# Two-layer diffusion backbone: the residual's latent rows are kept in DRAM during attention, the first output-weight unit is split early into their place, and GpSimd's subtracts leave the attention

## The chip, the cores and the metric

The kernel runs on one core of one Trainium2 chip. The metric is the device time of one execution in microseconds (us). The kernel before took 1191.76 us, the median of three runs (1187.81, 1191.76 and 1194.09). The core has five engines, each with a queue of its own that it serves in order: TensorE (PE in the profile, its weight loads PEld), VectorE (DVE), ScalarE (ACT), GpSimd (POOL) and SyncE (SP, which here issues the DMAs).

## The reference, cut to what matters

512 latent tokens and 256 context tokens of width 1024 go through two layers. Layer 0 mixes by pooling, layer 1 by attention with 8 query heads and 2 key/value heads of 128; each layer ends with a squared-ReLU MLP of width 4096. Only the latent stream leaves layer 1. The part around the change:

```python
# end of layer 0, both streams
x = x + gt2 * rms_norm(m_lat, g_mlp_post)
# layer 1
h_lat = modulate(rms_norm(x, g_mix_pre), sh1, sc1)
q_l, k_l, v_l = qkv_project(h_lat, w_qkv, g_q, g_k)      # and for the context
q_l, k_l = apply_axial_rope(q_l), apply_axial_rope(k_l)
s = einsum('bqhgd,bkhd->bhgqk', q, k) * HEAD_DIM ** -0.5  # 768 keys
p = softmax(s)
o = einsum('bhgqk,bkhd->bqhgd', p, v)
y_lat = o.reshape(B, L, D) @ w_o
x = x + gt1 * rms_norm(y_lat, g_mix_post)                 # residual: needs x again
m_lat = square(relu(modulate(rms_norm(x), sh2, sc2) @ w_mlp_in)) @ w_mlp_out
x = x + gt2 * rms_norm(m_lat, g_mlp_post)
```

The residual stream x is not needed between the normalisation that opens layer 1 and the addition behind the output projection.

## The kernel before, in words

Every fp32 operand of a large product is kept as two fp32r parts: hi is a rounded copy, lo is the operand minus hi. A product is then three matmuls (hi by hi, hi by lo, lo by hi). To make such a pair is called a split: one copy (ACT, or GpSimd) and one subtract (DVE, or GpSimd); `split`, lines 126 to 135, does it for a weight unit of 2048 columns, or for a quarter of one (512 columns) when `q` is given. With `pin` the two instructions keep the place that they have in the program.

The residual rows lie in one tile, `xr`, of six row blocks of 128 tokens: four latent (t = 0 to 3) and two context (4 and 5). It belongs to a pool, `residents`, on the right side of the on-chip memory together with `gate` and `junk`, which is closed while other tiles need the room (`held`), the rows going to the DRAM tile `spill` and back.

The order of the work is written by hand: `Steps` collects functions with planned times in us, sorts them by time and runs them, which emits the instructions. The framework then places the instructions that are not pinned by a simulated timeline (`TC_OPTS`, line 38), so what is ready earlier on an engine or on SP's queue may come ahead of what is written earlier. `last0` (line 1118) plans the end of layer 0 for the row blocks in the order 4, 5, 0, 1, 2, 3: residual add (`norm_r`), mean square (`norm_s`), scaled copy (`norm_c`), transposes with modulation (`norm_pair`), key/value projection (`kv_a` to `kv_c`), query projection (`q_a` at 67.851 to 104.478, `q_e`, `q_b` with the rotary products at line 1053). The attention's base is planned at 102.5, the output projection at 102.5 + 2.7 x 43.691.

`attention` has 32 steps of 2.7 planned us, head by head, four row blocks each. Step i computes scores (line 1204) into a two-bank PSUM tile (two of them), their negated maximum (DVE, line 1208), the exponential (ACT, line 1209) into one of four probability buffers `pbuf`, which are the first 768 columns of the two context row blocks of `xr`, of `gate` and of `acc`; the normalisation (line 1217 or 1219); six transposes (line 1229) whose results are split from PSUM (ACT line 1231, DVE line 1232); and, every second step, 18 matmuls of values by probabilities (line 1243), split again (lines 1245 and 1246). Transposes, query heads, values and projections share four PSUM banks.

The output weights w_o come in four units of 1 MB, (column half, row half), each loaded into one of three raw buffers and then split into a slot of the ring `aring` (line 1179): half of `hL` in `ra` (free once the query projections are done), `unit[0]`, `unit[1]`, `unit[2]`. The first two units are split in the attention, at steps 7 and 11.386, copy and subtract both on GpSimd and pinned:

```python
at(7, lambda: wo[0].append(wo_unit(0, 0, raws)))
at(7.01, lambda: split(*raws[0], True, True, True))
at(11.386, lambda: wo[0].append(wo_unit(0, 1, raws)))
at(11.396, lambda: split(*raws[1], True, True, True))
```

The other two go to slots that the attention itself uses and are split after it. `output` (line 1311) multiplies, evicts (`attn_ev`), adds the residual (`norm_r`, line 324), normalises, and starts the MLP; `mlp1` stores the four latent row blocks to `spill` (line 838), closes the residents, and gets the rows back before its end.

Of the kernel before, what the change touches and what calls it, by code (L numbers as in the profile page):

```python
# [9 lines left out]
F32 = mybir.dt.float32  # L10
F32R = mybir.dt.float32r
BF16 = mybir.dt.bfloat16
# [5 lines left out]
P = 128  # L18
D = 1024
# [21 lines left out]
class Steps:  # L41
# [3 lines left out]
    def at(self, t, fn, *args):  # L45
        self.items.append((t, len(self.items), fn, args))
# [7 lines left out]
def backbone(ctx: ExitStack, tc, x, c, ctx_in, c_ctx, w_ada, b_ada, g_mix_pre, g_mix_post,  # L54
# [10 lines left out]

    held = [ExitStack(), ExitStack()]

    def residents(stack):
        pool = stack.enter_context(tc.tile_pool(name="residents", bufs=1, side="right"))
        return (pool.tile([P, NT, D], F32, name="xr"), pool.tile([P, 2, D], F32, name="gate"),  # L70
                pool.tile([P, D], BF16, name="junk"))

    xr, gate, junk = residents(held[0])
    psA = ctx.enter_context(tc.tile_pool(name="psA", bufs=2, space=PSUM))
# [90 lines left out]
    def row_rstd(src):  # L165
        ss = sm_tile("ss")
        mean_square(src, ss, 0)
        return rstd(ss, 1)
# [151 lines left out]
    def gated(t, dst, src, n0, n1, pool=False):  # L320
        return (gp if pool else ve).tensor_tensor(out=dst[:, n0:n1], in0=src, in1=gate[:, slot[t], n0:n1], op=ALU.mult)  # L321

    def residual(t, y, n0=0, n1=D):
        ve.scalar_tensor_tensor(out=xr[:, t, n0:n1], in0=y[:, n0:n1], scalar=rs[t][:, 0:1],
                                in1=xr[:, t, n0:n1], op0=ALU.mult, op1=ALU.add)
# [157 lines left out]

    def norm_s(t, half=False):
        if not half:
            rs[t] = row_rstd(xr[:, t, :])
            return
        ss = sm_tile("ss")
        for h in range(2):
            mean_square(xr[:, t, 512 * h:512 * h + 512], ss, h)  # L490
        rs[t] = rstd(ss, 2)

    def norm_c(t, act, pool):
        r = rs[t][:, 0:1]
        if act:
            sc.activation(accv[:, t, :], xr[:, t, :], AF.Copy, scale=r)
        else:
            (gp if pool else ve).tensor_scalar(out=accv[:, t, :], in0=xr[:, t, :], scalar1=r, scalar2=None,
                                               op0=ALU.mult)

    turned = {}
# [333 lines left out]
    def mlp1(inner, last):  # L835
        nonlocal xr, gate, junk
        for t in range(NL):
            sy.dma_start(spill[:, t], xr[:, t])
        held[1].close()
        closing = ExitStack()  # L840
        pool = closing.enter_context(tc.tile_pool(name="pairs", bufs=1, side="right"))
# [276 lines left out]
    def last0(st, n, t):  # L1118
# [2 lines left out]
        st.at([8.8, 14, 19.2, 24.4, 29.6, 34.8][n], norm_r, t, (False, True, False, False, False, False)[n])  # L1121
        st.at([10, 16.738, 20.4, 25.6, 30.8, 36][n], norm_s, t, (False, False, False, False, True, False)[n])
        st.at([12, 17.906, 22.4, 27.6, 32.8, 36.716][n], norm_c, t, (True, True, True, True, True, True)[n], (False, False, False, False, False, False)[n])
        if n % 2:
            st.at([18.2, 28.6, 39][n // 2], norm_pair, t - 1, 1, 0, hH, hL, True, (True, True, False)[n // 2],
                  ((True, False, False, False, False, False, False, True), (True, True, True, False, False, False, True, True), (True, False, True, False, True, False, True, False))[n // 2])
# [49 lines left out]
    pTH = unit[2][:, 0:NT * LAT].rearrange("p (s n) -> p s n", n=LAT)  # L1176
    pTL = unit[1][:, 0:NT * LAT].rearrange("p (s n) -> p s n", n=LAT)
    pbuf = lambda i: (xr[:, 4, 0:TOK], xr[:, 5, 0:TOK], gate[:, 1, 0:TOK], acc[:, 4 * D:4 * D + TOK])[i]
    aring = Ring([ra[:, 8192:12288], unit[0], unit[1], unit[2]])

    def wo_unit(ch, kk, wait=None):
        return aring.load(w_o[0, 512 * kk:512 * kk + 512, 512 * ch:512 * ch + 512]
                          .rearrange("(k p) n -> p k n", p=P), 512, True, wait)

    steps = [(h, t) for h in range(NQ) for t in range(NL)]
# [95 lines left out]

    first1 = []

    def attention(st, base, unit_t):
        at = lambda i, fn, *args: st.at(base + unit_t * i, fn, *args)
        for i, (h, t) in enumerate(steps):
            if t == 0:
                at([-2, 3, 4.542, 7.928, 13.236, 15.602, 19.752, 23.755][h], q_head, h)
            at(i + 0.2, s_scores, i)
            at(i + 1.3, s_norm, i)  # L1290
            at(i + 3.1, s_turn, i)
            if t % 2:
# [111 lines left out]
```

## Time and profile before

| | |
|---|---|
| median of three runs | 1191.76 us |
| the profiled execution | 1193.66 us, of which the span is 1191.9 us |
| busy: PE, DVE, ACT, POOL | 1149.0, 941.9, 643.8, 74.5 us |
| DMA | 147.88 MB, mean 124 GB/s |

In a timeline a row is: start in us, duration in us, engine, line, operation, out<-in, partitions x elements, and "xN" when N like instructions in a row are taken together (the duration is then from the first start to the last end). In square brackets stands how long the engine was idle before it and what released it. Durations of neighbours overlap a little, since an engine begins an instruction before the one ahead of it has left it; from start to start is what an instruction costs. In a table of stretches a row holds the busy us of each engine with instruction counts, the clock that TensorE was granted (1.00 is full), the DMA share and GB/s.

### The profile page before, as it was taken

How to read it: one execution, taken by the hardware profiler on the slowest of the kernel's cores; microseconds unless marked ns; L12 is line 12 of the kernel's file. 1: busy time of each engine (PE TensorE's matmuls, PEld its weight loads, DVE VectorE, ACT ScalarE, POOL GpSimd, SP SyncE). 2: the span in 40 equal slices, each digit the busy share in tenths (PEclk: the TensorE clock that was granted, in tenths of full speed). 3: DMA queues.
4: the chain of work that ended last, by engine and by line, in shares of the span. 5: the costliest groups of instructions: out<-in, count | busy, mean ns of one | idle time of the engine just before them, and what ended most of it. 6: DMA issues, size and time to landing. Idle time of an engine off the chain costs nothing.

```text
span 1191.9 us, 15641 instructions
## 1 busy us (share of the span) xinstructions
PE 1149.0 (96%) x6026; PEld 993.8 (83%) x6026; DVE 941.9 (79%) x1521; ACT 643.8 (54%) x1141; POOL 74.5 (6%) x88
## 2 busy tenths in 40 slices
PE   6889999999999999999989989999899999999997
PEld 5568989899889888998867879998888888888886
DVE  5666686889989898998786589978677788778876
ACT  4676665445345534555775347872677346435523
POOL 1010000000000000000221232001000000000000
PEclk9899999999999999999998989999999999999999
DMA  9993222334434444344422111006244133314302
GB/s 339 389 319 121 72 75 102 118 130 142 157 126 142 141 140 144 107 155 138 166 71 79 64 36 37 1 6 207 108 140 145 39 135 123 113 47 142 106 31 111
DMA packets 92985, 147.88 MB, mean 124 GB/s; under 512 B 2752, under 2 KB 67824, under 8 KB 92912
## 3 DMA queue, kind: packets, MB, share of 16 engines
q1 hardware_dynamic: 92912, 146.90, 36.1%
q8 instruction: 47, 0.77, 0.3%
q14 instruction: 26, 0.21, 0.1%
HBM read 139.55 MB, written 7.34 MB: 123 GB/s over the span
## 4 chain that ended last, share of the span: by engine, by line
issue 45%; PE 43%; DVE 4%; ACT 3%; DMA 2%; POOL 2%; POOLq 0%; DVEq 0%; SPq 0%; ACTq 0%
PE psin L566 14%; PE pso L886 11%; PE psy L1269 3%; PE psq L1028 3%; PE po L1243 3%; PE pss L1204 2%; PE pspool L465 2%; PE pso L783 1%; PE pspt L1229 1%; ACT junk L157 1%; DMA raw<-in_w_ada 1%; POOL rs L162 1%; PE psada L229 1%; POOL rs L1037 1%; DVE work L321 1%
## 5 line engine op out<-in xcount | busy, mean ns | idle before, releaser
L783 PE MATMUL pso<-units,rb 128*128 128x512 f32 x1152 | 277.0, 392 | 0.0
L783 PEld LDWEIGHTS pso<-units,rb 128*128 128x128 f32 x1152 | 214.9, 188 | 41.7
L268 DVE SCALAR_TENSOR_TENSOR rows<-raw,cond,rows 128x256 f32<-128x256 f32 x280 | 123.0, 482 | 0.7
L795 DVE TENSOR_TENSOR acc<-acc,pso 128x512 f32<-128x512 f32 (+1 forms) x133 | 87.6, 675 | 34.5 <-PE pso L783 34.2
L566 PE MATMUL psin<-ra,rb 128*128 128x512 f32 (+2 forms) x384 | 103.2, 363 | 2.6 <-ACT ra L363 1.6
L162 POOL TENSOR_TENSOR rs<-ss,nhalf 128x1 f32<-128x1 f32 x42 | 27.1, 646 | 954.2 <-ACT ss L158 951.0
L886 PE MATMUL pso<-units,pairs 128*128 128x512 f32 x336 | 82.5, 389 | 0.0
L566 PEld LDWEIGHTS psin<-ra,rb 128*128 128x128 f32 x384 | 69.9, 192 | 13.1 <-ACT ra L535 1.9
L566 PE MATMUL psin<-ra 128*128 128x512 f32 x256 | 80.6, 389 | 0.0
L886 PEld LDWEIGHTS pso<-units,pairs 128*128 128x128 f32 x336 | 63.1, 188 | 13.1
L890 DVE TENSOR_TENSOR acc<-acc,pso 128x512 f32<-128x512 f32 x72 | 48.6, 681 | 29.0 <-PE pso L886 29.0
L677 PE MATMUL psin<-ra,units 128*128 128x384 f32 x336 | 65.7, 337 | 0.4 <-ACT psin L689 0.4
L677 PE MATMUL psin<-sums,units 128*128 128x384 f32 x336 | 63.6, 336 | 0.0
L677 PEld LDWEIGHTS psin<-ra,units 128*128 128x128 f32 x336 | 59.7, 188 | 3.1 <-ACT psin L689 0.5
L677 PEld LDWEIGHTS psin<-sums,units 128*128 128x128 f32 x336 | 59.0, 188 | 1.3
L566 PEld LDWEIGHTS psin<-ra 128*128 128x128 f32 x256 | 48.1, 188 | 10.0
L566 PE MATMUL psin<-rb 128*128 128x512 f32 (+1 forms) x144 | 53.5, 372 | 0.3 <-DVE rb L364 0.2
L1028 PE MATMUL psq<-units,ra 128*128 128x512 f32 x216 | 52.0, 393 | 0.0
L566 PE MATMUL psin<-rb,ra 128*128 128x512 f32 x128 | 49.8, 389 | 0.0
L122 DVE TENSOR_TENSOR units<-raw,units 128x1024 fp32r<-128x1024 f32 x34 | 41.2, 1216 | 9.7 <-ACT units L121 9.6
L1028 PEld LDWEIGHTS psq<-units,ra 128*128 128x128 f32 x216 | 40.1, 188 | 8.4 <-DVE ra L364 0.2
L793 ACT COPY acc<-pso 128x512 f32<-128x512 f32 x44 | 24.6, 586 | 35.8 <-PE pso L783 35.7
(271 smaller groups left out, 2379.8 us busy)
## 6 DMA issues: line engine op xcount, KB each, us to landing
raw<-in_w_ada SPq DMA_DIRECT2D x48, 1024.0 KB, 5.3
raw<-in_w_mlp_in SPq DMA_DIRECT2D x32, 1024.0 KB, 5.3
raw<-in_w_mlp_out SPq DMA_DIRECT2D x32, 1024.0 KB, 5.9
raw<-in_w_qkv SPq DMA_DIRECT2D x6, 1024.0 KB, 5.2
spill<-xr SPq DMA_DIRECT2D x10, 512.0 KB, 8.6
xr<-spill SPq DMA_DIRECT2D x10, 512.0 KB, 6.8
raw<-in_w_o SPq DMA_DIRECT2D x4, 1024.0 KB, 5.4
xr<-in_x SPq DMA_DIRECT2D x4, 512.0 KB, 4.9
```

What stands on the lines that cost most here:

```text
L122: ve.tensor_tensor(out=lo[:, z], in0=raw[:, z], in1=hi[:, z], op=ALU.subtract)):
L162: gp.tensor_tensor(out=r[:, 0:1], in0=ss[:, parts + 3:parts + 4], in1=nhalf[:, 0:1], op=ALU.pow)
L268: ve.scalar_tensor_tensor(out=r, in0=raw[:, k, :], scalar=cond[:, k, c:c + 1], in1=r, op0=ALU.mult, op1=ALU.add)
L566: te.matmul(ps[:, bank, o:o + ln], w[:, k, fs], a[:, k, t0:t0 + ln], start=(k == 0 and n == 0), stop=(k == KT - 1 and n == 2))
L677: te.matmul(bank, w[k], a[k], start=start and k == 0 and m == 0, stop=stop and k == 3 and m == 2, skip_group_check=True)
L783: te.matmul(pss[h][:, 0:cols[h][1]], a[:, f, ts_], w[:, f, cols[h][0]:sum(cols[h])], start=(n == 0 and not seeded[t]), stop=(n == len(seq) ...
L795: ve.tensor_tensor(out=d, in0=d, in1=ps[:, 0:w], op=ALU.add)
L886: te.matmul(ps, a, w, start=(m == 0), stop=(m == len(seq) - 1))
L890: ve.tensor_tensor(out=M[n][:, t], in0=M[n][:, t], in1=ps, op=ALU.add)
L1028: te.matmul(ps, a[:, k, sl], w[:, k % 4, :], start=(k == 0 and n == 0), stop=(k == KT - 1 and n == 2))
L1243: te.matmul(po[:, 0:256], v[:, kt, hs], p[:, kt, qs], start=(kt == 0 and n == 0), stop=(kt == NT - 1 and n == 2))
L1269: te.matmul(ps, a[:, k, sl], w[:, k % 4, o:o + width], start=(k == 0 and n == 0), stop=(k == KT - 1 and n == 2))
```

## The change

- `xr` becomes an object of two tiles: `ctx` holds the two context row blocks, `lat` the four latent ones in a pool of its own, `latents`. `lend()` closes that pool and opens a tile of the same size, `lent`, in its place.
- At the end of layer 0 each latent row block is stored to `spill`, planned at 22.5, 27.7, 33 and 37.
- The ring of the output weights is now `lent`, the half of `hL`, `unit[1]`, `unit[2]`. Its first load calls `lend()`.
- The first unit is loaded at step -6.8 and split in quarters at steps -5.2, -4.4, -3.6 and -2.8, during the query projections, on ACT and DVE, not pinned.
- The second unit is loaded at step 3 and split in quarters at steps 22.9, 24.9, 26.9 and 28.9: the copy on GpSimd, the subtract on DVE, pinned.
- At step 36.9 `back` loads the four row blocks from `spill` into places that are free by then: the two context row blocks of `xr` and the last two of `acc`. `xrow(t)` gives the place of a row block; the residual add, the normalisation and the store in `mlp1` use it.

The diff, cut to its core:

```diff
+    class Rows:
+        def __init__(self, stack):
+            pool = stack.enter_context(tc.tile_pool(name="residents", bufs=1, side="right"))
+            self.ctx = pool.tile([P, NT - NL, D], F32, name="xr")
...
+            self.lat = self.open().tile([P, NL, D], F32, name="xl")
+        def open(self):
+            return self.stack.enter_context(tc.tile_pool(name="latents", bufs=1, side="right"))
...
+        def lend(self):
+            self.close()
+            return self.open().tile([P, NL * D], F32R, name="lent")
...
+    away = {}
+    def xrow(t):
+        return away[t] if t in away else xr[:, t, :]
     def residual(t, y, n0=0, n1=D):
-        ve.scalar_tensor_tensor(out=xr[:, t, n0:n1], in0=y[:, n0:n1], scalar=rs[t][:, 0:1],
-                                in1=xr[:, t, n0:n1], op0=ALU.mult, op1=ALU.add)
+        x_ = xrow(t)[:, n0:n1]
+        ve.scalar_tensor_tensor(out=x_, in0=y[:, n0:n1], scalar=rs[t][:, 0:1], in1=x_, op0=ALU.mult, op1=ALU.add)
...
         for t in range(NL):
-            sy.dma_start(spill[:, t], xr[:, t])
+            sy.dma_start(spill[:, t], xrow(t))
+        away.clear()
...
+        if t < NL:
+            st.at([0, 0, 22.5, 27.7, 33, 37][n], lambda t: sy.dma_start(spill[:, t], xr[:, t]), t)
...
-    aring = Ring([ra[:, 8192:12288], unit[0], unit[1], unit[2]])
+    aring = []
     def wo_unit(ch, kk, wait=None):
-        return aring.load(w_o[0, 512 * kk:512 * kk + 512, 512 * ch:512 * ch + 512]
+        if not aring:
+            aring.append(Ring([xr.lend(), ra[:, 8192:12288], unit[1], unit[2]]))
+        return aring[0].load(w_o[0, 512 * kk:512 * kk + 512, 512 * ch:512 * ch + 512]
...
+    def back():
+        for t in range(NL):
+            away[t] = xr[:, NL + t, :] if t < 2 else accv[:, NL + t - 2, :]
+            sy.dma_start(away[t], spill[:, t])
...
-        at(7, lambda: wo[0].append(wo_unit(0, 0, raws)))
-        at(7.01, lambda: split(*raws[0], True, True, True))
-        at(11.386, lambda: wo[0].append(wo_unit(0, 1, raws)))
-        at(11.396, lambda: split(*raws[1], True, True, True))
+        at(-6.8, lambda: wo[0].append(wo_unit(0, 0, raws)))
+        for q in range(4):
+            at((-5.2, -4.4, -3.6, -2.8)[q], lambda q: split(*raws[0], False, False, False, q), q)
+        at(3, lambda: wo[0].append(wo_unit(0, 1, raws)))
+        for q in range(4):
+            at((22.9, 24.9, 26.9, 28.9)[q], lambda q: split(*raws[1], True, True, False, q), q)
+        at(36.9, back)
```

More of the change, by code (lines that the diff above doesn't have):

```diff
@@ L66, in backbone, with close, __getitem__ @@
     held = [ExitStack(), ExitStack()]
+    class Rows:
+        def __init__(self, stack):
+            pool = stack.enter_context(tc.tile_pool(name="residents", bufs=1, side="right"))
+            self.ctx = pool.tile([P, NT - NL, D], F32, name="xr")
+            self.gate, self.junk = pool.tile([P, 2, D], F32, name="gate"), pool.tile([P, D], BF16, name="junk")
+            self.stack = ExitStack()
+            stack.callback(self.close)
+            self.lat = self.open().tile([P, NL, D], F32, name="xl")
+        def open(self):
+            return self.stack.enter_context(tc.tile_pool(name="latents", bufs=1, side="right"))
+        def close(self):
+            self.stack.close()
+        def lend(self):
+            self.close()
+            return self.open().tile([P, NL * D], F32R, name="lent")
+        def __getitem__(self, key):
+            t = key[1]
+            return self.lat[key] if t < NL else self.ctx[(key[0], t - NL) + tuple(key[2:])]
     def residents(stack):
-        pool = stack.enter_context(tc.tile_pool(name="residents", bufs=1, side="right"))
-        return (pool.tile([P, NT, D], F32, name="xr"), pool.tile([P, 2, D], F32, name="gate"),
-                pool.tile([P, D], BF16, name="junk"))
+        rows = Rows(stack)
+        return rows, rows.gate, rows.junk
     xr, gate, junk = residents(held[0])
@@ L485, in norm_s @@
         if not half:
-            rs[t] = row_rstd(xr[:, t, :])
+            rs[t] = row_rstd(xrow(t))
             return
@@ L489, in norm_s @@
         for h in range(2):
-            mean_square(xr[:, t, 512 * h:512 * h + 512], ss, h)
+            mean_square(xrow(t)[:, 512 * h:512 * h + 512], ss, h)
         rs[t] = rstd(ss, 2)
@@ L495, in norm_c @@
         if act:
-            sc.activation(accv[:, t, :], xr[:, t, :], AF.Copy, scale=r)
+            sc.activation(accv[:, t, :], xrow(t), AF.Copy, scale=r)
         else:
-            (gp if pool else ve).tensor_scalar(out=accv[:, t, :], in0=xr[:, t, :], scalar1=r, scalar2=None,
+            (gp if pool else ve).tensor_scalar(out=accv[:, t, :], in0=xrow(t), scalar1=r, scalar2=None,
                                                op0=ALU.mult)
```

## The prediction

> **What bounds the kernel now.** The page comes first: the span, and the fortieths with the clock that TensorE was granted.
>
> ```profile
> span 1191.9 us, 15641 instructions
> ...
> PEclk9899999999999999999998989999999999999999
> ```
>
> A fortieth is 29.8 us; the clock shows 8 in the 24th, 685 to 715 us. TensorE (PE) is busy nearly everywhere, so time can only be won where PE stands or runs at a low clock. The change touches the layer-0 end, the attention and the output projection (about 600 to 860 us), so I read the stages in there.
>
> ```profile
> 655.00:688.00 33.00, 33.00 (x149) 27.19 (x149) 19.51 (x35) 11.15 (x51) 9.40 (x13) 1.00 0.19 64
> 702.00:709.00 7.00, 2.21 (x8) 1.44 (x9) 7.00 (x9) 2.86 (x6) 2.42 (x1) 0.67 0.49 149
> 709.00:714.50 5.50, 5.50 (x21) 5.31 (x22) 4.54 (x10) 2.15 (x6) 0.00 (x0) 0.50 0.00 1
> ...
> 760.00:780.00 20.00, 20.00 (x154) 19.68 (x152) 17.12 (x34) 16.79 (x36) 2.14 (x1) 1.00 0.01 1
> ```
>
> Columns: stretch, its length, busy us of PE, weight loads, DVE, ACT and POOL, then the granted clock and DMA. Attention in full swing (760 to 780) is bound by PE: 20.00 of 20.00, with DVE at 17.12. But at its start there is a hole. From 702 to 709 PE works 2.21 us of 7 while DVE is busy all 7, and from 709 to 714.5 PE is busy all the time, but at clock 0.50. The timelines of POOL, DVE and PE show why.
>
> ```profile
> 602.47 0.62 POOL L129 CAST units<-raw 128x512 fp32r<-128x512 f32 x1
> 697.75 1.90 POOL L129 CAST ra<-raw 128x2048 fp32r<-128x2048 f32 x1
> 699.72 4.70 POOL L132 TENSOR_TENSOR ra<-raw,ra 128x2048 fp32r<-128x2048 f32 x1
> 725.28 4.86 POOL L132 TENSOR_TENSOR rb<-raw,rb 128x2048 fp32r<-128x2048 f32 x1
> ```
>
> ```profile
> 692.21 0.74 DVE L1053 TENSOR_TENSOR work<-work,acc 128x256 f32<-128x256 f32 x2
> 699.09 5.61 DVE L1053 TENSOR_TENSOR work<-work,acc 128x256 f32<-128x256 f32 x2
> 704.63 0.55 DVE L1232 TENSOR_TENSOR units<-pspt,units 128x384 fp32r<-128x384 f32 x1
> ```
>
> ```profile
> 705.23 1.11 PE L1192 MATMUL pq<-ident,acc 128*128 128x128 f32 x4 [3.50 <-DVE units L1232]
> 707.31 0.87 PE L1229 MATMUL pspt<-ident,gate 128*128 128x128 f32 x3 [0.97 <-DVE units L1232]
> 708.77 2.29 PE L1204 MATMUL pss<-rb 128*128 128x384 f32 x6 [0.59 <-ACT acc L1209]
> ...
> 711.35 2.27 PE L1204 MATMUL pss<-rb 128*128 128x384 f32 x6
> ...
> 714.55 2.45 PE L1243 MATMUL po<-units,rb 128*128 128x256 f32 x18
> ```
>
> The pair of rotary products at L1053, 0.74 us a step earlier, lasts 5.61 us here and ends at 704.70, just after GpSimd's subtract of the first output-weight unit ends at 704.42. DVE takes its work in order, so the eviction L1232 that PE's banks wait for comes only at 704.63, and PE waits 3.50, 0.97 and 0.59 us. After that it runs at half clock up to the first probability-by-value products at 714.55. The second unit's subtract at 725.28 does the like on a smaller scale.
>
> **The change part by part.**
>
> *The first unit leaves GpSimd and the attention.* The stall itself: 5.61 - 0.74 = 4.87 us of DVE. From 699 to 709 nothing else held DVE up, so all that hangs on it moves up by 4.87 us, and the score set of 708.77 starts at 703.90. Next the clock. Between 708.77 and 714.55 lie two score sets of six products and nine transposes, 5.78 us. The same work in mid-attention:
>
> ```profile
> 760.57 0.49 PE L1229 MATMUL pspt<-ident,gate 128*128 128x128 f32 x3
> 760.82 1.29 PE L1204 MATMUL pss<-rb,units 128*128 128x384 f32 x6
> 761.95 0.49 PE L1229 MATMUL pspt<-ident,gate 128*128 128x128 f32 x3
> 762.27 0.82 PE L1229 MATMUL pspt<-ident,acc 128*128 128x128 f32 x6
> 762.85 2.40 PE L1243 MATMUL po<-units,rb 128*128 128x256 f32 x18
> ```
>
> By starts: a score set 761.95 - 760.82 = 1.13, three transposes 0.25, six 0.58. Two sets and nine transposes make 2 x 1.13 + 0.25 + 0.58 = 3.09 us, so the half clock costs 5.78 - 3.09 = 2.69 us, and I let that go with the idle time that I hold to cause it. What is late next is ACT's exponential of step 4, whose end frees the score bank for the set at 711.35:
>
> ```profile
> 709.44 0.94 ACT L1209 ACTIVATE xr<-pss,sm 128x768 f32<-128x768 f32 x1
> ```
>
> It ends at 710.38, or 4.87 earlier at 705.51. PE at full clock would want it at 703.90 + 1.13 + 0.25 = 705.28, so PE waits 0.23 us. Sum of this part: 4.87 + 2.69 - 0.23 = 7.3 us gained. Its upper bound is all three waits (5.06), the clock (2.69) and about 1 us for the transposes of 705.23 to 708.77, whose 1.11 and 0.87 us for four and three stand against 0.49 for three: 8.8 us.
>
> [...]
>
> *The first unit's new split* is four ACT casts and four DVE subtracts of 512 columns, planned 14 to 8 us ahead of the attention's base.
>
> ```profile
> 798.22 4.30 DVE L132 TENSOR_TENSOR units<-raw,units 128x512 fp32r<-128x512 f32 x7 [1.12 <-ACT units L129]
> ```
>
> One subtract takes 4.30 / 7 = 0.61 us, the four 2.45, and four casts on ACT I put at the 0.6 us of GpSimd's 602.47 row, so 2.5. The cover is 655 to 688, where DVE is busy 19.51 of 33 us and ACT 11.15: cost nothing. Without that cover it would be 2.45.
>
> *The second unit.* GpSimd's 4.86 us subtract goes. What it cost shows here:
>
> ```profile
> 728.31 2.23 DVE L1217 TENSOR_SCALAR xr<-xr,sm 128x768 f32<-128x768 f32 x1
> ...
> 731.73 0.60 DVE L1217 TENSOR_SCALAR gate<-gate,sm 128x768 f32<-128x768 f32 x1
> ```
>
> ```profile
> 731.86 0.55 PE L1229 MATMUL pspt<-ident,xr 128*128 128x128 f32 x3 [0.19 <-DVE ra L1246]
> ```
>
> DVE lost 2.23 - 0.60 = 1.63 us and PE waited 0.19. In exchange DVE gets four subtracts of 0.61 us, two steps apart, at steps 22.9 to 28.9, held at their places by the pin, each behind a GpSimd cast of 0.62 us. They fall into the stretch of the 760 to 780 row, where DVE has 20.00 - 17.12 = 2.88 us to spare for 2.45. Bounds for the new cost: 0 (all in the gaps) and 2.45 (all passed on to PE). The nearest row is 731.86, where 1.63 us in one lump cost 0.19, so four single pieces cost about 0.2. Won and lost cancel: 0. Behind each subtract on DVE stand the evictions and maxima of the steps, and PE waits for those.
>
> *The latent rows.* Four stores of 512 KB at the end of layer 0 and four loads after the attention, all on SP.
>
> ```profile
> spill<-xr SPq DMA_DIRECT2D x10, 512.0 KB, 8.6
> xr<-spill SPq DMA_DIRECT2D x10, 512.0 KB, 6.8
> ```
>
> ```profile
> 612.01 0.37 SPq L1008 DMA_DIRECT2D acc<-in_rope  x1
> 643.71 0.37 SPq L107 DMA_DIRECT2D raw<-in_w_qkv  x1
> ```
>
> Each store waits for DVE's residual add of its rows, and SP serves in order, so whatever is queued behind it waits too: the last rotary-table load, if the row block 2 store comes ahead of it, and otherwise the query-weight load, for which SP stands free from 612.01 to 643.71.
>
> ```profile
> 612.48 1.27 DVE L324 SCALAR_TENSOR_TENSOR xr<-work,rs,xr 128x1024 f32<-128x1024 f32 x1
> ...
> 615.77 0.76 DVE L1017 TENSOR_TENSOR acc<-acc,grow 128x256 f32<-128x256 f32 x2 [0.51 <-DMA acc<-in_rope]
> ```
>
> That add is over at 613.75, so the table would be asked for 613.75 + 0.37 - 612.01 = 2.1 us later, and DVE already waits 0.51 us for it. Bounds: 0 and 2.1. The plan puts the table loads at 18.4 and the store at 33, so I take 0. The last store is planned at 37 and the first copy into the lent place at 102.5 - 5.2 x 2.7 = 88.5, some 50 us of plan for a store of 8.6. The loads have this room:
>
> ```profile
> 792.75 0.98 PE L1229 MATMUL pspt<-ident,acc 128*128 128x128 f32 x6
> ```
>
> ```profile
> 821.27 1.28 DVE L324 SCALAR_TENSOR_TENSOR xr<-acc,rs,xr 128x1024 f32<-128x1024 f32 x1 [0.47 <-POOL rs L162]
> ```
>
> The last transposes that read the probability rows end by 793.73; row block 0 is needed at 821.27, 27 us later, and a load lands in 6.8. Cost nothing; without the room, 6.8. The later stores for the MLP are the same four from other places. The address arithmetic in `residual`, `norm_s` and `norm_c` issues the same instructions.
>
> **Sum:** 7.3 + 0 - 0 = 7.3 us. The profiled execution took 1193.66 us (span 1191.9), 1.9 above the median of the runs; I expect 1186.4 in its terms, and **1191.76 - 7.3 = 1184.5 us** for the median.
>
> **The rivals.**
>
> *The clock stays low.* Even without the stall PE waits at the attention's start. It is free from 705.23 - 3.50 = 701.73; up to the score set at 703.90 it has seven transposes to do, 7 x 0.25 / 3 = 0.58 us, and idles the other 1.6; with the 0.23 above that is 1.8 of 3.8 us. Another place shows what split idling can do:
>
> ```profile
> 854.02 1.53 PE L349 MATMUL psx<-ident,acc 128*128 128x128 f32 x12 [1.76 <-DVE acc L498]
> 857.19 0.50 PE L566 MATMUL psin<-ra,rb 128*128 128x256 f32 x2 [1.64 <-ACT ra L363]
> ```
>
> ```profile
> 850.00:860.00 10.00, 6.38 (x43) 5.74 (x43) 6.25 (x10) 6.84 (x12) 0.55 (x1) 0.90 0.14 55
> ```
>
> Waits of 1.76 and 1.64 us with transposes between them brought the clock to 0.90 over that stretch. If it falls here too, the 2.69 us stay: 7.3 - 2.7 = 4.6 gained, 1187.2. Against it: the single waits are no longer than the 1.64 us one, and shorter by half in sum. [...]
>
> *Nothing happens.* The 5.61 us could be a wait of L1053 for something else, or the new plan of the engines' order could bring another delay to the same place: 1191.8. Against it: DVE's rows show no releaser there, and the two ends lie 0.28 us apart.
>
> *DVE becomes the bound in steps 23 to 29, and it ends slower.* Mechanism: each pinned subtract waits its whole cast (0.62), takes 0.61, and the next cast locks out a normalisation (0.62): 4 x 1.85 = 7.4 us of DVE, against 2.88 to spare. At the attention's start 4.87 us of lost DVE time cost PE 7.3 with the clock, a factor 1.5. If nothing of it found a gap, 7.4 x 1.5 = 11.1 us are lost and 7.3 won: 1191.76 + 3.8 = 1195.6. It decides from 7.3 / 1.5 = 4.9 us of uncovered DVE time. For it: DVE is at 86% there. Against it: GpSimd has one other instruction in 760 to 780, so its casts can run ahead of the subtracts; the 1.63 us lump cost only 0.19.
>
> **How the numbers follow.** The forecast gets 0.63, the low clock 0.24, no change 0.07, the slower case 0.06. The forecast's own range goes from the bound of 8.8 plus 0.2 (1182.8) to 7.3 less 2.1 for the table (1186.6). The range reaches through the low clock with 2.1 for the table and 1.6 of passed-on subtracts (4.6 - 3.7 = 0.9 gained, 1190.9); I round to 1182 and 1191. A measurement of this kernel can tell about 0.5%, 6.0 us, from no change, so faster means under 1185.8. Four fifths of the forecast's case lie under that (0.50), and a tenth or two of the low clock's (0.04): 0.54. Slower by that much is only the far part of the slower case and bad luck beside it: 0.05. The rest, 0.41, is within.
>
> **What would show it.** Right: no L1053 pair over 1 us at the attention's start; no GpSimd TENSOR_TENSOR of 2048 columns there; PE's first values products some 7 us earlier after the last projection, with the clock at 1.00 in the 12 us before; GpSimd casts of 0.62 us and DVE subtracts of 0.61 us in the second half of the attention without PE waits over 0.3 us beside them; four loads landed before the first residual add of the output stage. Wrong: a clock of 0.5 remains in front of the first values products (the low clock); L1053 or another DVE instruction is still long (nothing happens); PE waits for L1232 and DVE near 100% in steps 23 to 29 (the slower case); DVE waiting for the table or a latent row.

## The result and the profile after

The changed kernel takes 1185.35 us (median of 11 runs, 1181.69 to 1189.93) against 1191.76 us (11 runs, 1187.81 to 1195.28): a ratio of 0.9949 with a 95% interval of 0.9929 to 0.9968, so 6.1 us gained (3.8 to 8.5). The forecast was 1184.5. The profiled execution took 1182.18 us, against 1193.66 before. First the page of the kernel after.

```profile
span 1180.4 us, 15674 instructions
...
PEclk9999999999999999999999999999999999999999
```

The 8 that stood in the 24th fortieth is gone. Next the attention's head: the timeline of DVE, then that of PE, from the first score set to the first value products at 703.14 (lines have moved by 22 to 32: L1053 is L1081 now, L1204 is L1236, L1229 is L1261, L1232 is L1264, L1243 is L1275).

```profile
694.85 0.75 DVE L1081 TENSOR_TENSOR work<-work,acc 128x256 f32<-128x256 f32 x2
...
716.71 0.61 DVE L1249 TENSOR_SCALAR xr<-xr,sm 128x768 f32<-128x768 f32 x1
```

```profile
683.81 1.23 PE L1236 MATMUL pss<-rb 128*128 128x384 f32 x6
...
698.21 0.52 PE L1261 MATMUL pspt<-ident,gate 128*128 128x128 f32 x3 [0.28 <-DVE units L1264]
699.67 1.34 PE L1236 MATMUL pss<-rb 128*128 128x384 f32 x6 [0.94 <-ACT acc L1241]
700.84 0.49 PE L1261 MATMUL pspt<-ident,gate 128*128 128x128 f32 x3
701.42 1.31 PE L1236 MATMUL pss<-rb 128*128 128x384 f32 x6
...
703.14 2.40 PE L1275 MATMUL po<-units,rb 128*128 128x256 f32 x18
```

The pair that lasted 5.61 us takes 0.75, and the normalisation that lasted 2.23 us takes 0.61. PE's longest wait in the head is 0.94 us where it was 3.50, and a score set lasts 1.3 us where it lasted 2.29. The table of stretches says the same of the clock (columns as in the prediction).

```profile
700.00:710.00 10.00, 9.92 (x72) 9.54 (x71) 9.45 (x21) 8.58 (x20) 0.33 (x1) 1.00 0.01 2
750.00:760.00 10.00, 9.98 (x78) 9.67 (x76) 9.66 (x19) 8.91 (x19) 2.08 (x4) 1.00 0.01 2
```

The second row is where GpSimd's casts and the subtracts of the second unit have gone: DVE is busy 9.66 of 10 us, PE 9.98.

To compare the profiles stage by stage, all times below are starts of PE: the first score set, the first value products (18 matmuls into `po`) and the first output product (into `psy`). The *head* lies between the first two, the *body* between the second and third, the *rest* from there to the end of the span. The first scores start at 688.05 before and 683.81 after, but the code ahead of that point that could matter is costed below, and most of this difference is not the change's (last section).

| | first scores | head | body | rest |
|---|---|---|---|---|
| before | 688.05 | 26.50 | 85.36 | 391.99 |
| after | 683.81 | 19.33 | 84.79 | 392.47 |

Head 7.17 us won, body 0.57 won, rest 0.48 lost: 7.26 us from the first scores on, where the forecast was 7.3.

### The profile page after: what moved, and what is told of

Read it like the earlier page. It is cut to its first block, busy times and chain, and to the rows that moved or that the text cites. A ratio compares the mean times of both kernels' runs of the same rounds, so it can differ in the third digit from the quotient of the medians.

```text
span 1180.4 us, 15674 instructions
## 1 busy us (share of the span) xinstructions
PE 1141.3 (97%) x6026; PEld 987.0 (84%) x6026; DVE 939.2 (80%) x1529; ACT 645.4 (55%) x1145; POOL 64.0 (5%) x88
```

## The experiments

The theory: GpSimd's 2048-column subtract, which reads on-chip memory, holds a DVE instruction with two inputs there until it has itself ended (in the kernel before the pair lasts 5.61 us and ends 0.28 us behind the subtract); at the head PE depends on what DVE has queued behind that, waits (3.50 us the longest), and then runs at clock 0.50. Rivals: the gain comes from the rest of the change (rows in DRAM, another ring, a new emitted order); GpSimd's traffic into the memory does it, not its reading; or such a subtract costs the same wherever it stands. All runs in one table, with the stages of each one's profile; ratios are to the kernel before on the same chip.

| run | first scores | head | body | rest | time, us | ratio (95%) |
|---|---|---|---|---|---|---|
| e1 after again | 685.63 | 19.33 | 84.79 | 392.45 | 1184.29 | 0.9948 (0.9929 to 0.9967) |
| e12 after, third time | 686.40 | 19.36 | 84.82 | 392.82 | 1185.41 | 0.9949 (0.9927 to 0.9970) |
| e2 DVE in place | 684.81 | 19.74 | 89.33 | 390.52 | 1187.32 | 0.9977 (0.9958 to 0.9997) |
| e3 rows only | 683.51 | 26.40 | 85.50 | 390.89 | 1189.36 | 0.9991 (0.9973 to 1.0010) |
| e4 second on GpSimd | 690.00 | 19.33 | 84.47 | 392.40 | 1186.28 | 0.9964 (0.9941 to 0.9986) |
| e6 first on GpSimd, early | 690.04 | 19.91 | 84.10 | 392.55 | 1187.87 | 0.9963 (0.9943 to 0.9983) |
| e7 one lone subtract | 687.20 | 24.21 | 84.84 | 391.05 | 1188.08 | 0.9957 (0.9940 to 0.9975) |
| e11 two lone subtracts | 683.59 | 27.98 | 84.83 | 391.00 | 1193.26 | 1.0017 (0.9999 to 1.0034) |
| e8 a lone write | 685.28 | 19.36 | 84.82 | 392.44 | 1187.69 | 0.9941 (0.9921 to 0.9960) |
| e5 first in quarters | 685.75 | 21.42 | 85.29 | 390.54 | 1185.15 | 0.9933 (0.9914 to 0.9952) |
| e9 both in quarters | 691.10 | 20.55 | 84.92 | 390.53 | 1186.28 | 0.9953 (0.9933 to 0.9973) |
| e10 first one later | 687.38 | 19.36 | 87.55 | 392.01 | 1186.40 | 0.9960 (0.9944 to 0.9976) |

One head in this table is not like the others. In e6 325 of the 336 projection products into `psq` start ahead of the first scores, in all other profiles 312, so its head lacks 13 products that the others have in it.

**The change again (e1, e12).** No edit.

> The changed kernel once more, as the yardstick for the runs beside it. Measured in the trace is the head of the attention: from the start of the first score set (line 1204 before, 1236 here) to the start of the first value products (1243, here 1275). It was 714.55 - 688.05 = 26.50 us before and 703.14 - 683.81 = 19.33 us after. The lock theory (GpSimd's two-input subtract keeps DVE's two-input products waiting, PE idles, its clock halves) expects the head again within 0.5 us of 19.33, clock 1.00 in it, and 6 to 7 us less than before in time. The low-clock rival expects some executions with a head about 2.7 us longer: 22.

> The kernel after once more, as the yardstick on the same chip for the others of this call: 6 us below before (4 to 8.5), head of 19.3 us from first scores to first value products, the rotary pair at 0.75 us.

Three timings on three occasions give 0.9949, 0.9948 and 0.9949, and the head is 19.33 or 19.36 us each time: the gain is real and sits where it was forecast. What differs between these profiles is the time *ahead* of the first scores, by 2.6 us, in the same code.

**The rows and the ring, without the moved subtracts (e3).**

```diff
-        at(-6.8, lambda: wo[0].append(wo_unit(0, 0, raws)))
-        for q in range(4):
-            at((-5.2, -4.4, -3.6, -2.8)[q], lambda q: split(*raws[0], False, False, False, q), q)
-        at(3, lambda: wo[0].append(wo_unit(0, 1, raws)))
-        for q in range(4):
-            at((22.9, 24.9, 26.9, 28.9)[q], lambda q: split(*raws[1], True, True, False, q), q)
+        at(7, lambda: wo[0].append(wo_unit(0, 0, raws)))
+        at(7.01, lambda: split(*raws[0], True, True, True))
+        at(11.386, lambda: wo[0].append(wo_unit(0, 1, raws)))
+        at(11.396, lambda: split(*raws[1], True, True, True))
```

> The changed kernel with the old splits put back (both units whole, cast and subtract on GpSimd, steps 7 and 11.386): only the rows' way through DRAM, the new ring and the reload are left of the change. The lock theory expects the kernel before: a head of 26.5 us within 0.5, the rotary pair at 5.6 us, the same time within 0.2%; the rows themselves cost nothing. The rival that the gain comes from the rows or from where the tiles lie expects a head near 19.3 and some 6 us won.

Its DVE, GpSimd and PE at the head:

```profile
694.55 5.51 DVE L1081 TENSOR_TENSOR work<-work,acc 128x256 f32<-128x256 f32 x2
```

```profile
695.18 4.59 POOL L154 TENSOR_TENSOR lent<-raw,lent 128x2048 fp32r<-128x2048 f32 x1
```

```profile
700.59 1.12 PE L1224 MATMUL pq<-ident,acc 128*128 128x128 f32 x4 [3.40 <-DVE units L1264]
...
704.12 2.29 PE L1236 MATMUL pss<-rb 128*128 128x384 f32 x6 [0.58 <-ACT acc L1241]
```

The old picture to the tenth: long pair, subtract ending beside it (699.77 and 700.06), the 3.40 us wait, the 2.29 us score set. The time is that of before. So the rows in DRAM and the new ring win nothing by themselves; the first rival falls. They also cost nothing that can be measured.

**Only the subtracts moved to DVE, in their old places (e2).**

```diff
-        at(7.01, lambda: split(*raws[0], True, True, True))
+        at(7.01, lambda: split(*raws[0], True, True, False))
-        at(11.396, lambda: split(*raws[1], True, True, True))
+        at(11.396, lambda: split(*raws[1], True, True, False))
```

> The kernel before with one thing changed: the subtracts of the first two output-weight units go to DVE, in their old places and in one piece; GpSimd keeps the casts, the rows stay where they are. If it were enough to free GpSimd, the head would be about 19.3 us. The lock theory expects only a part: the cast (1.90 us, it reads the on-chip memory) can still hold up the pair of rotary products, and then a 2.3 us subtract stands in DVE's queue ahead of the evictions that PE waits for, so DVE loses about 2.3 to 4 us in place of 4.87: a head of 21 to 25 us, 1 to 5 us won in time. If the gain came from the rows' place alone, the head stays at 26.5.

DVE of this run, at the head and in mid-attention; then GpSimd; then PE.

```profile
695.85 1.16 DVE L1053 TENSOR_TENSOR work<-work,acc 128x256 f32<-128x256 f32 x2
...
706.88 2.29 DVE L132 TENSOR_TENSOR ra<-raw,ra 128x2048 fp32r<-128x2048 f32 x1
...
716.17 2.35 DVE L1217 TENSOR_SCALAR xr<-xr,sm 128x768 f32<-128x768 f32 x1
```

```profile
694.50 1.89 POOL L129 CAST ra<-raw 128x2048 fp32r<-128x2048 f32 x1
...
716.21 1.90 POOL L129 CAST rb<-raw 128x2048 fp32r<-128x2048 f32 x1
```

```profile
719.97 2.30 PE L1243 MATMUL po<-units,rb 128*128 128x256 f32 x17 [1.17 <-DVE units L1232]
```

The head falls to 19.74 us, better than expected, since DVE took up its own 2.29 us subtract only behind the head. But the body grows from 85.36 to 89.33 us: whole 2.29 us subtracts in DVE's queue, and a GpSimd *cast* that holds a normalisation from 0.61 to 2.35 us (they end 0.41 us apart); behind the latter PE waits 1.17 us. So 6.8 us won and 4.0 lost. Taking the subtract off GpSimd wins the head; what the rest of the change is good for is the room to do the subtracts in small pieces and where DVE has time.

**One lone subtract put back, then two, then a write alone (e7, e11, e8).** The kernel after, plus work that nobody needs: a GpSimd subtract of 2048 columns that reads the finished parts of the first unit and writes columns that are free; then two of them; then three fills of the same columns, which read nothing.

```diff
+        def extra():
+            z = unit[0][:, 2048:4096]
+            hi, lo = raws[0][1:]
+            tc.keep_in_program_order(gp.tensor_tensor(out=z, in0=hi, in1=lo, op=ALU.subtract))
+        at(2.03, extra)
+        at(2.04, extra)
```

The last line is there in e11 alone. In e8 the body of `extra` is `for n in range(3): tc.keep_in_program_order(gp.memset(z.bitcast(F32), 0.0))`.

> The changed kernel with the suspected cost put back alone: one GpSimd subtract of 2048 columns with two on-chip inputs (the two parts of the first unit), written to a place that nothing reads, at the head of the attention. No weight, row or load is moved by it. The lock theory expects the whole loss to come back: a rotary pair of about 5 us (line 1081), head 25 to 27 us, 6 to 7 us more time than the changed kernel. If the gain had to do with the splits' data, their buffers or the plan, nothing happens: head 19.3.

> The kernel after with two lone GpSimd subtracts of 2048 columns, one behind the other, at the attention's head. They read the first unit's finished parts and write columns that nobody reads until later; nothing else waits for them, the output is the reference's. One such subtract lengthened the head from 19.3 to 24.2 us in its profile. If GpSimd's reading holds DVE for a whole instruction each time, two lengthen it further, to 26 to 32 us, because a second DVE instruction with two inputs in SBUF is held for up to 4.6 us, and the time rises 5 to 10 us over the kernel after. If only the first hold counts because DVE makes the second up, the head stays at 24 to 25 us and the time 3 to 5 us over the kernel after.

> The same place, but GpSimd only writes: three fills of the same 2048 columns, one after another, which read nothing (about 4 to 6 us together). If it is GpSimd's reading that keeps DVE's second input out, the rotary pair stays at 0.75 us and the head near 19.3, with at most one of DVE's normalisations or copies held up. If any GpSimd work on the on-chip memory blocks DVE, the pair takes 4 us or more and the head is as long as with the subtract, 25 to 27 us.

Each run's GpSimd work and the rotary pair beside it, e7 first, then e11 with PE's wait, then e8.

```profile
696.91 4.56 POOL L1338 TENSOR_TENSOR rb<-lent 128x2048 fp32r<-128x2048 f32 x1
```

```profile
698.25 3.85 DVE L1081 TENSOR_TENSOR work<-work,acc 128x256 f32<-128x256 f32 x2
```

```profile
693.30 9.20 POOL L1338 TENSOR_TENSOR rb<-lent 128x2048 fp32r<-128x2048 f32 x2
```

```profile
694.63 8.15 DVE L1081 TENSOR_TENSOR work<-work,acc 128x256 f32<-128x256 f32 x2
```

```profile
703.30 1.12 PE L1224 MATMUL pq<-ident,acc 128*128 128x128 f32 x4 [6.03 <-DVE units L1264]
```

```profile
694.98 5.55 POOL L1339 MEMSET rb<- 128x2048 f32 x3
```

```profile
696.33 0.75 DVE L1081 TENSOR_TENSOR work<-work,acc 128x256 f32<-128x256 f32 x2
```

This settles the mechanism. One subtract holds the pair for 3.85 us (it started 1.34 us ahead of the pair, so less of it was left than in the kernel before), two hold it for 8.15, longer than one of them lasts (9.20 together), and the pair ends 0.3 us behind the last. The fills keep GpSimd busy for 5.55 us at the same place and hold nothing: 0.75. So writing alone did not do it here, and the subtract's reading is what is left. Against the kernel after timed beside it (e12), e11 is slower by 1193.26 - 1185.41 = 7.9 us, with a head 8.6 us longer: as forecast for two. For e7 the head is 4.9 us longer, under the expectation, and its time can't be told from e8's.

**GpSimd again, but in quarters and elsewhere (e4, e6).** In the kernel after, the second unit's subtracts (e4), or the first unit's whole split (e6), go back to GpSimd at the change's own places.

```diff
-            at((22.9, 24.9, 26.9, 28.9)[q], lambda q: split(*raws[1], True, True, False, q), q)
+            at((22.9, 24.9, 26.9, 28.9)[q], lambda q: split(*raws[1], True, True, True, q), q)
```

```diff
-            at((-5.2, -4.4, -3.6, -2.8)[q], lambda q: split(*raws[0], False, False, False, q), q)
+            at((-5.2, -4.4, -3.6, -2.8)[q], lambda q: split(*raws[0], False, True, True, q), q)
```

> The changed kernel with the subtracts of the second unit on GpSimd again, in quarters at their new steps 22.9 to 28.9. Head unchanged at 19.3. In steps 22 to 30 each quarter (about 1.6 us by the 512-column rows of GpSimd) can hold up a normalisation of 0.6 us on DVE, while DVE is relieved of 4 x 0.61 us. The lock theory expects PE waits of 0.2 us or less at each and a time within 0.1% of the changed kernel. The rival that DVE is the bound in these steps expects about 0.5 to 2.4 us less time than the changed kernel.

> The changed kernel with the first unit's early quarters given to GpSimd, cast and subtract, during the query projections. The lock theory says that the place decides and not the engine: DVE's two-input instructions there (rotary products, lines 1081 to 1086) are held up by up to 1.6 us each, but DVE has slack of some 13 us in 33 and PE does not wait: head 19.3 within 0.7 us, time within 0.1% of the changed kernel. The rival that any GpSimd subtract beside the projections and attention costs expects 2 to 7 us more.

In time neither differs from the kernel after by more than the intervals allow, but the profiles tell them apart. In e4 the body is 0.31 us shorter, and all of it lies where the subtracts are: from the fourth group of value products to the first output product PE takes 66.20 us, as before the change, against 66.51 in after and e1. There the four subtracts on DVE cost PE 0.31 us, and those on GpSimd, with all that they hold up, nothing that shows.

In e6 the sum is what counts, since its first scores come 13 projection products later. From the same projection product (the 201st into `psq`) to the first output product it takes 132.89 us, the kernel after 130.01: 2.9 us more, where nothing was expected. For this place the profile speaks for the rival of 2 to 7 us, which the timing cannot decide. It need not be a hold: a small GpSimd result (`rs`, line 1065) now stands behind the quarters in GpSimd's queue, and DVE waits 3.58 us for it where it waited 1.18; and PE's order has changed as well. These causes are not separated.

**The old place, in quarters (e5, e9).** The kernel before with `split` called for each quarter `q`, on GpSimd at 7.01, and in e9 at 11.396 too; nothing else.

```diff
-        at(7.01, lambda: split(*raws[0], True, True, True))
+        for q in range(4):
+            at(7.01, lambda q: split(*raws[0], True, True, True, q), q)
```

> The kernel before with the first unit's split in its old place cut into four quarters, cast and subtract on GpSimd as before (the same columns, the same engine, four shorter instructions). If the subtract locks DVE out for a whole instruction, DVE waits at most for one quarter at a time (about 1.2 to 1.6 us) and gets its turn between them: the pair of rotary products (line 1053) lasts 1.5 to 3 us in place of 5.61, and the head 20 to 23 us in place of 26.5. If GpSimd's work only slows DVE by sharing bandwidth, the pair stays at some 5 us and the head at 26.

> The kernel before with both units' GpSimd copies and subtracts in quarters of 512 columns, at the old places. The first unit's quarters gave 5.1 us of head and ran as fast as the full change; the second unit's quarters should win what is left there: if each hold lasts one piece (1.3 to 1.6 us), the DVE normalisation of 2.24 us beside it falls to about 1.2 to 1.6 us and PE wins 0 to 0.8 us, so a time 5 to 8 us below before. If short pieces only spread the same sum of holds, nothing is won by it: the time is that of the first unit's quarters alone, 5 to 7 us below before, or a little longer.

PE of e5 and then of e9 at the same instructions:

```profile
701.34 0.52 PE L1229 MATMUL pspt<-ident,gate 128*128 128x128 f32 x3 [1.47 <-ACT units L1231]
702.53 2.29 PE L1204 MATMUL pss<-rb 128*128 128x384 f32 x6 [0.67 <-ACT acc L1209]
```

```profile
706.70 0.52 PE L1229 MATMUL pspt<-ident,gate 128*128 128x128 f32 x3 [1.48 <-ACT units L1231]
707.89 1.31 PE L1204 MATMUL pss<-rb 128*128 128x384 f32 x6 [0.68 <-ACT acc L1209]
```

Quarters at the old place win 5.1 and 6.0 us of the head, as a pair held for a short piece lasts 1.67 us (1.68 in e9) instead of 5.61. The second unit's quarters took 0.4 us off the body. In time both are as good as the full change, and neither can be told from it. The two excerpts hold the surprise: the same waits to 0.01 us, once followed by half clock (2.29 us for six products), once by full clock (1.31).

**The whole subtract, moved behind the head (e10).** Two lines of the kernel before: the load is asked for later, and of the engines GpSimd alone gets another order.

```diff
-        at(7, lambda: wo[0].append(wo_unit(0, 0, raws)))
-        at(7.01, lambda: split(*raws[0], True, True, True))
+        at(8.4, lambda: wo[0].append(wo_unit(0, 0, raws)))
+        at(8.41, lambda: split(*raws[0], True, True, True))
```

> The kernel before with one move: the load and the GpSimd copy and subtract of the first unit are planned at step 8.4 instead of 7, so that on GpSimd they stand behind the normalisation of step 7; all other engines keep their order. Both whole subtracts then run back to back in mid-attention, some 10 to 22 us behind the first value products. If what costs is GpSimd's reading beside the rotary pair at the attention's head, the pair there takes 0.75 us, the head from first scores to first value products 19 to 20 us instead of 26.5, with the clock at 1.00, and the time falls by some 6 us as with the full change; the subtracts each hold one or two DVE instructions up by 1.6 to 4 us there, which costs PE 0.2 to 1 us each. If such a subtract costs the same wherever it stands, most of the 7 us is lost again behind the head and the time stays within 2 us of before.

Its GpSimd subtracts, and the normalisations of DVE beside them:

```profile
717.42 4.86 POOL L132 TENSOR_TENSOR ra<-raw,ra 128x2048 fp32r<-128x2048 f32 x1
...
724.52 4.86 POOL L132 TENSOR_TENSOR rb<-raw,rb 128x2048 fp32r<-128x2048 f32 x1
```

```profile
720.45 2.24 DVE L1217 TENSOR_SCALAR xr<-xr,sm 128x768 f32<-128x768 f32 x1
...
727.10 2.69 DVE L1217 TENSOR_SCALAR acc<-acc,sm 128x768 f32<-128x768 f32 x1
```

And PE behind them:

```profile
731.57 1.01 PE L1229 MATMUL pspt<-ident,acc 128*128 128x128 f32 x6 [0.60 <-DVE ra L1246]
...
734.14 1.07 PE L1243 MATMUL po<-units,rb 128*128 128x256 f32 x7 [0.49 <-DVE units L1232]
```

The head drops to 19.36 us, that of the full change, and the body grows by 2.2 us: the first subtract holds a normalisation for 2.24 us, as the second did in the kernel before, and the second one, pushed back, holds another for 2.69 us, and PE waits 0.44, 0.60 and 0.49 us behind that. Net 4.95 us by the stages, 4.8 timed (2.9 to 6.7). The same subtract costs 7.1 us at the head and about 2 behind the head: the third rival falls as well. No version beat the kernel after beyond its interval, but this small move comes within 1.0 us of it on the same chip.

## Why the prediction was right, point by point

*The head (forecast 7.3, measured 7.17).* The steps came out one by one. The first scores start 688.05 - 683.81 = 4.24 us earlier in the profile after; with that added, the score set forecast for 703.90 started at 699.67 + 4.24 = 703.91, the next one, forecast for 705.51, at 701.42 + 4.24 = 705.66, and the value products, forecast for 714.55 - 7.33 = 707.22, at 707.38. The wait for ACT came where it was forecast: the exponential of step 4 ends at 701.27 + 4.24 = 705.51, to the hundredth, and the three transposes ahead of the last set take 701.42 - 700.84 = 0.58 us by starts where 0.25 is usual, so PE lost 0.33 there, not 0.23. The 0.94 us wait is the old one of 0.59: the set still starts 1.46 us behind the three transposes ahead of it (708.77 - 707.31 and 699.67 - 698.21), but these now last 0.52 us and not 0.87.

*The clock (the rival with 0.24).* It stayed at 1.00 in the head of every profile with the subtract gone from there and the waits of 0.28 and 0.94 left (after, e1, e4, e8, e10, e12). The rival's mechanism is real all the same: e5 lost the clock behind waits of 1.47 and 0.67 us. The two listed waits make 1.22 us where the rival had 1.6 + 0.23. Six profiles are few, but the last section gives a measured reason to think that this was not luck.

*First unit split early (forecast 0).* The profile after has the early split, that of e3 has not. From the same projection product into `psq` to the first scores (630.35 to 683.81, and 630.05 to 683.51) both take 53.46 us. So it cost nothing, as forecast.

*Second unit (forecast: 0.2 won, 0.2 lost).* This was mis-sized. The fourth group of value products starts at 733.71 in the kernel before:

```profile
733.71 2.31 PE L1243 MATMUL po<-units,rb 128*128 128x256 f32 x18
```

It moved up by 12.29 us, to 721.42, the first group by 11.41: 0.88 won, not the 0.19 of the one wait that the profile showed. PE beside that wait, before and then after:

```profile
731.18 0.49 PE L1229 MATMUL pspt<-ident,xr 128*128 128x128 f32 x3
731.86 0.55 PE L1229 MATMUL pspt<-ident,xr 128*128 128x128 f32 x3 [0.19 <-DVE ra L1246]
732.55 1.31 PE L1204 MATMUL pss<-rb,units 128*128 128x384 f32 x6
```

```profile
719.72 0.82 PE L1261 MATMUL pspt<-ident,xr 128*128 128x128 f32 x6
720.29 1.29 PE L1236 MATMUL pss<-rb,units 128*128 128x384 f32 x6
```

By starts the six transposes took 732.55 - 731.18 = 1.37 us and take 0.57 now: 0.80 won at this one place. A listed wait counts only from the end of the instruction ahead, and so misses what the broken overlap costs; the prediction had used starts for the clock, and should have here. From there to the output projection 0.31 was lost again, against 0.2 forecast; the rival that DVE becomes the bound came close (9.66 of 10 us busy), but PE was busy 9.98 of the same 10. Its 0.62 us of hold behind each cast hardly showed: the four casts ran in one row ahead of the subtracts, from 749.79 to 752.07, and the one normalisation beside them lasted 0.70 us where 0.61 is usual. Elsewhere casts of 512 columns did hold DVE: in e6, beside four of them, a pair at L1081 lasted 1.13 us, and 0.49 just before.

*The rows (forecast 0).* SP of the kernel after:

```profile
608.74 0.37 SPq L1036 DMA_DIRECT2D acc<-in_rope  x1
610.49 10.24 SPq L1153 DMA_DIRECT2D spill<-xl  x2
...
776.68 1.15 SPq L1319 DMA_DIRECT2D xr<-spill  x2
781.82 0.32 SPq L1319 DMA_DIRECT2D acc<-spill  x1
```

```profile
809.53 1.28 DVE L352 SCALAR_TENSOR_TENSOR xr<-acc,rs,xr 128x1024 f32<-128x1024 f32 x1 [0.47 <-POOL rs L184]
```

The last table load went out 1.75 us ahead of the store it could have been stuck behind, as assumed, though DVE now waits 0.77 us for it and not 0.51. Of the four loads one went out at 653.90 already, the others at 776.68 to 781.82; they landed 3.7 to 4.1 us later, over 23 us ahead of the first residual add, whose wait is still the same 0.47 us for GpSimd. Experiment e3, which has all of this, is the time of before.

*Not foreseen: the output projection.* Its products whose piece of w_o lies in the lent place are slower. The rows for that line in the kernel after, then before:

```profile
L1301 PE MATMUL psy<-lent,ra x48: 393/396/477, 787.9 to 818.1; 128*128 128x512 f32 x48
```

```profile
L1269 PE MATMUL psy<-ra x48: 389/389/478, 799.9 to 829.7; 128*128 128x512 f32 x48
```

Median 396 against 389 ns, 48 times: 0.34 us. Every run with `lent` has it (e1, e3, e4, e6, e7, e8, e11, e12), none without. Why is open.

*From 7.3 to 6.1.* The stages give 7.26 us, the timing 6.1 (3.8 to 8.5). The difference lies inside the interval. One candidate is argued, not shown: the rest is 1.4 to 1.9 us longer where the clock dips near 850 us. Stretches of e10 and then of e3:

```profile
850.00:860.00 10.00, 8.20 (x51) 7.91 (x52) 8.61 (x11) 7.27 (x12) 0.00 (x0) 0.83 0.14 40
```

```profile
850.00:860.00 10.00, 8.14 (x63) 7.61 (x64) 7.99 (x11) 8.22 (x13) 0.00 (x0) 1.00 0.01 3
```

By the table seven profiles that keep the clock at the head have this longer rest (after, e1, e4, e6, e8, e10, e12), while e2 and e9 keep it and don't; of those that lose the clock at the head, e3, e5, e7 and e11 don't have it, but before does. If the kernel before mostly behaves like e3, some 1.5 us of the gain is given back there. Where the dips of the runs without a profile lie is not known. How long they are in sum is: the granted clock of every run is on record, and half clock lasts 2 x (1 - clock) x span (the profiles of before and after show 1.00 and 0.50 and nothing between). That is 26.3 us in the mean of the 35 runs of the kernel before that were timed with e1, and 19.7 us in the 12 of e1: 6.6 us less (standard error 1.9), where the head alone has 10.2 us less in the two profiles (three pieces, none). So in the mean about one piece of 3.4 us seems to have come back somewhere, which agrees with the candidate; with that error it is not shown.

## What to carry to other kernels

When an instruction takes several times its usual time (here 5.61 us for 0.74) and the trace gives no releaser, look at the other engines' ends: a GpSimd instruction that reads on-chip memory and ends beside it (here 0.28 us ahead) is the suspect, and a copy of it that does nothing useful, placed there again, proves it. What it cost here depended on what was queued behind the held instruction: one subtract cost 7 us at the head, where PE waited on DVE's queue and then lost its clock, and about 2 in the body. So first try to move it by one place in its queue, or to cut it in four: with either, the time could not be told from that of the large change. But look at what else waits for the engine that gets the pieces, as e6 shows.

## What the runs showed of the hardware

*A cast holds DVE as well.* In e2 a normalisation, which has one tensor input and a column of scalars, lasted 2.35 us in place of 0.61 and ended 0.41 us behind the 1.90 us cast beside it. So this hold needed neither the subtract nor two tensor inputs.

*The half clock comes in pieces of about 3.4 us.* Rows of stretches, first of the kernel after, then of e3.

```profile
620.00:630.00 10.00, 6.29 (x31) 5.28 (x30) 5.85 (x16) 7.72 (x23) 3.29 (x7) 0.83 0.14 54
```

```profile
700.00:710.00 10.00, 7.87 (x29) 6.91 (x29) 9.02 (x18) 5.15 (x11) 0.00 (x0) 0.50 0.34 105
```

A mean of 0.83 over 10 us is 0.17 x 10 / 0.5 = 3.4 us at half clock, and the value comes back at several places; e3's head has three such pieces, 10.2 us. In the kernel after, half clock sets in at 82.73, 625.45, 847.32 and 1178.41 us, the last three 159, 224 and 321 times 3.413 us behind the first; in the kernel before at 32.01, 55.90, 86.62, 625.93, 704.44, 858.03 and 1189.13 us, 7, 16, 174, 197, 242 and 339 times. So within each of these two profiles all pieces begin on one grid of 3.41 us, and the 10 us stretches of ten others (e1, e3 to e7, e9 to e12) fit such a grid to their last digit. Against the work it lies differently from profile to profile: the three transposes behind the wait of 1.47 us start 2.33 us into a stretch of the grid in e5 and, behind 1.48, 2.69 us into one in e9. That fits the pair. Stretches cut along the grid of each, e5 first:

```profile
699.01:702.43 3.42, 1.38 (x11) 0.93 (x9) 3.42 (x6) 2.52 (x6) 3.33 (x4) 1.00 0.00 0
702.43:705.84 3.41, 3.31 (x11) 3.22 (x12) 3.41 (x8) 2.14 (x6) 1.63 (x1) 0.50 0.15 8
```

```profile
704.01:707.43 3.42, 1.73 (x14) 1.28 (x13) 3.42 (x7) 2.17 (x4) 3.34 (x4) 1.00 0.00 0
707.43:710.84 3.41, 2.84 (x15) 2.37 (x15) 3.41 (x8) 2.62 (x7) 1.98 (x2) 1.00 0.03 10
```

The same waits fall differently into these stretches. In e5 PE is busy 1.38 of 3.42 us in one of them, and half clock follows; in e9 it is busy at least 1.73 in each, and none follows. In the head of the kernel after PE is busy at least 2.18 us in any stretch of 3.41, wherever the grid may lie, so a loss like e5's was not near. The busy share alone does not decide it: in the kernel after PE is busy 1.57 of 3.41 us from 840.49 on and full clock follows, and 1.56 us in the next stretch, from 843.90 on, and half clock follows. Nor did it take one long wait: in e5 1.47 and 0.67 us were enough.

*Most of the spread between runs goes with the clock.* Up to the first scores the code of before, e2, e5, e9 and e10 is the same, and these start at 684.81 to 691.10 us. A profile with dips only at 80 and 620 us (after, e3, e11) starts them at 683.5 to 683.8; the others, with more dips between 10 and 70 us or longer ones behind 620, are later by 1 to 7.5 us. The runs without a profile say the same: over the 35 of the kernel before that were timed with e1, time and half clock go together (correlation 0.94, 0.44 us more for each us at half clock). That alone does not make the clock the cause: the idle time ahead of a half clock (1.47 and 0.67 us in e5) also costs by itself. The spread is as large as the change itself, and a comparison of two profiles must therefore be made stage by stage.
